# An encoder layer on one core: the later half of the in-projection in another order, the attention output loaded into its pages, and rows loaded after gates

## The chip, the cores and the metric

The kernel runs on one core of one Trainium2 chip. The metric is the device time of one execution in microseconds, as the median of several runs. Durations of single instructions come from one profiled execution.

## The reference, cut to what matters

One layer of a hybrid encoder over 2048 rows of 1024 features, in float32:

```
h  = rms_norm(x) * norm_mix
z  = h @ w_in          # q_a | k_a | v_a | q_b | k_b | v_b | gate_a | gate_b
y_a = windowed grouped-query attention of q_a, k_a, v_a
y_b = neighbourhood attention of q_b, k_b, v_b on a 32 x 64 grid
x  = x + (sigmoid(gate_a) * (y_a @ w_proj_a) + sigmoid(gate_b) * (y_b @ w_proj_b)) @ w_out
x  = x + relu(rms_norm(x) * norm_mlp @ w_up)^2 @ w_down
out = rms_norm(x) * norm_final
```

## The kernel before, in words

Every float32 operand is split into a high part, cast by ScalarE (L282 for most, L178 for a weight slice), and a low part, the rest, which VectorE subtracts (L283, L179). A product is then three matmuls of 128x512 (L286 to L288, or L202 to L204). The big products are done as seven block products (numbered 1 to 7, as in Strassen's scheme), whose operands are sums of blocks.

**In-projection.** h is kept transposed in "pages" of SBUF. QUADS lists groups of columns of w_in; each group (a "quad") does its seven products against the rows of one half of the sequence: quads 0 to 8 for the first half, quads 9 to 13 for the second. A quad of 256 columns has two groups of 12 matmuls per product, the one of 128 columns (O_KA) has one. After product 1 the bank is copied by ScalarE (L532), and product 6 goes on in the copy. Results leave through the three `ze` tiles to DRAM (`qs_a`, `qs_b`, `ks_a` and so on; L427 to L432 fill them, L452 stores). Beside quads 5 to 7 a generator `h1_sums` reads four slices of the second half's h back from DRAM (`h1d`), scales them on ScalarE (L552), sums on VectorE and stores through GpSimd. Beside quads 9 to 12, `wo_parts` prepares the blocks of w_out (`wo_d`).

**Attention.** Then come attention A and B. TensorE alternates between attention work (scores L1049, transposes L1077, products L1089) and "filler": gate tiles for the second half, then `proj_tiles`, which multiply y_a by w_proj_a. The transposed probabilities `pt` of attention B are cast by ScalarE (`phb`, L1083) and their rest taken by VectorE (`plb`, L1084). `paced` decides when the next piece of filler is issued. y_a is taken from DRAM by `y_page`: a 0.5 MB load into a `raw` tile (L940), then the cast L282 and the subtraction L283 into two pages.

**Gates and out-projection.** For each half m, `gated(f)`, f from 0 to 7, loads a row of gates and of A's product (`z`, L1544 and L1546), does 8 groups of 12 matmuls over two calls, combines on VectorE (L1553), and adds into m0 to m3 (L279). `out_products` then multiplies by w_out, with `pgl` tiles loaded from `wo_d` (L1451), copies four banks after product 1 (L1491) and adds the rest to rows of x (`xr`, loaded by `x_row`, 0.5 MB each, added by L279). At m = 1 the rows of m = 0 are normalised and turned beside the gates (`ht`, L249 and L254), and the first operands of the up-projection are prepared (`uraw`, `ubh`).

What sets the order: the program is built with a scheduler that takes each engine's instructions into one fixed order; an engine then works strictly in that order. `tc.issue_after(i)` tells it to place the enclosed instructions behind instruction i, without a wait of its own. DMAs are issued by the engine in whose order they stand, mostly SyncE (SP), some by ScalarE and GpSimd.

## Time and profile before

| what | us |
|---|---|
| median of 3 runs (2633.69 to 2640.96) | 2635.83 |
| the profiled execution, whole | 2633.67 |
| its span, first to last instruction | 2631.9 |
| TensorE busy (97%) | 2556.9 |
| VectorE busy (65%) | 1708.3 |
| ScalarE busy (50%) | 1308.2 |
| mean granted TensorE clock | 0.993 |

TensorE is busy for nearly the whole span, so what can be read from the profile are the places where it stands still, what it waits for there, and the granted clock around them. The views used are the waits by stage, tables of busy time by stretch, the chain of work in time order, and single rows of the timeline.

### The profile page before, as it was taken

The page shows a single profiled execution, that of the slowest core. Times are in us where ns is not written, and L with a number is a line of the kernel's source. Part 1 is how long each engine was busy: PE and PEld are TensorE (multiplying, and loading weights), DVE is VectorE, ACT ScalarE, POOL GpSimd, SP SyncE. Part 2 cuts the span into 40 slices and gives each one's busy share as a digit, 9 for nine tenths or more (in the row PEclk, how much of TensorE's full clock was granted, in tenths as well). Part 3 has the DMA queues.
Part 4 walks back from the last instruction along what each step waited for, and adds up shares of the span by engine and source line. Part 5 has one row for each costly group of instructions (what it writes and reads, how often), then busy time and mean ns, then how long its engine had stood idle before and what let it go on. Part 6 is the DMA issues. An engine that isn't in the chain of part 4 may idle for free.

```text
span 2631.9 us, 34511 instructions
## 1 busy us (share of the span) xinstructions
PE 2556.9 (97%) x11936; PEld 2123.0 (81%) x11936; DVE 1708.3 (65%) x2696; ACT 1308.2 (50%) x2345; POOL 335.1 (13%) x460
## 2 busy tenths in 40 slices
PE   8999999999998989989999999999999999999998
PEld 6877888878887878878777888888887888888887
DVE  7857476656664666656787677776656634554766
ACT  7365464567775666514246555644444322323444
POOL 1001001143445645200000000000000000000011
PEclk9999999999999989999999999999999999999999
DMA  5768578783358888797897655854427825444554
GB/s 184 224 181 296 163 246 269 256 246 113 96 150 207 228 250 233 232 330 245 266 331 248 232 209 199 284 199 145 155 97 291 313 102 183 147 145 168 184 195 165
DMA packets 348160, 553.22 MB, mean 210 GB/s; under 512 B 30904, under 2 KB 152888, under 8 KB 345808
## 3 DMA queue, kind: packets, MB, share of 16 engines
q1 hardware_dynamic: 333520, 515.35, 60.4%
q10 hardware_dynamic: 10944, 24.12, 2.5%
q0 software_dynamic: 3520, 11.54, 1.2%
q8 instruction: 94, 1.54, 0.2%
q14 instruction: 82, 0.67, 0.1%
HBM read 364.19 MB, written 186.71 MB: 209 GB/s over the span
## 4 chain that ended last, share of the span: by engine, by line
PE 78%; DMA 10%; DVE 6%; ACT 3%; issue 2%; SPq 2%; POOL 0%; DVEq 0%; ACTq 0%; POOLq 0%
PE b L287 16%; PE b L288 16%; PE b L286 16%; PE zb L286 5%; PE zb L288 5%; PE zb L287 5%; PE mm L202 2%; PE mm L204 2%; PE mm L203 2%; PE av L1089 1%; DMA h2d<-ht 1%; PE pt L863 1%; DMA y_b<-yb 1%; PE pt L1077 1%; PE s L1049 1%
## 5 line engine op out<-in xcount | busy, mean ns | idle before, releaser
L287 PE MATMUL b<-dwh,dah 128*128 128x512 f32 x896 | 348.7, 389 | 0.4 <-DVE dwh L283 0.4
L288 PE MATMUL b<-dwh,dah 128*128 128x512 f32 x896 | 347.8, 389 | 0.0
L286 PE MATMUL b<-dwh,dah 128*128 128x512 f32 x896 | 338.5, 389 | 1.7 <-ACT dwh L282 1.7
L282 ACT CAST dah<-da 128x1024 fp32r<-128x1024 f32 (+1 forms) x128 | 120.9, 945 | 367.4 <-PE b L288 246.7
L286 PE MATMUL zb<-zh,zwhl 128*128 128x512 f32 x728 | 286.2, 393 | 7.1 <-ACT zb L532 3.7
L287 PE MATMUL zb<-zh,zwhl 128*128 128x512 f32 x728 | 285.9, 393 | 0.0
L288 PE MATMUL zb<-zh,zwhl 128*128 128x512 f32 x728 | 284.0, 391 | 0.8 <-DVE zwhl L283 0.8
L283 DVE TENSOR_TENSOR dah<-da,dah 128x1024 fp32r<-128x1024 f32 (+1 forms) x128 | 139.2, 1089 | 217.5 <-ACT dah L282 215.8
L286 PE MATMUL b<-ubh,uwhlb 128*128 128x512 f32 x592 | 231.4, 391 | 5.1 <-ACT uwhlb L282 3.5
L287 PE MATMUL b<-ubh,uwhlb 128*128 128x512 f32 x592 | 231.0, 390 | 0.0
L288 PE MATMUL b<-ubh,uwhlb 128*128 128x512 f32 x592 | 229.1, 389 | 0.0
L286 PEld LDWEIGHTS b<-dwh,dah 128*128 128x128 f32 x896 | 168.1, 188 | 36.9 <-ACT dwh L282 2.1
L287 PEld LDWEIGHTS b<-dwh,dah 128*128 128x128 f32 x896 | 168.2, 188 | 35.8 <-DVE dwh L283 0.8
L288 PEld LDWEIGHTS b<-dwh,dah 128*128 128x128 f32 x896 | 168.2, 188 | 34.9
L279 DVE TENSOR_TENSOR uc<-b,uc 128x512 f32<-128x512 f32 x160 | 109.3, 689 | 119.4 <-PE b L288 112.8
L286 PEld LDWEIGHTS zb<-zh,zwhl 128*128 128x128 f32 x728 | 137.2, 188 | 39.6 <-ACT zb L532 4.9
L202 PE MATMUL mm<-zh,whl 128*128 128x512 f32 x368 | 158.5, 431 | 3.3 <-ACT z L470 2.2
L288 PEld LDWEIGHTS zb<-zh,zwhl 128*128 128x128 f32 x728 | 137.4, 189 | 29.7 <-DVE zwhl L283 1.6
L287 PEld LDWEIGHTS zb<-zh,zwhl 128*128 128x128 f32 x728 | 137.4, 189 | 27.6
L204 PE MATMUL mm<-zh,whl 128*128 128x512 f32 x368 | 146.1, 397 | 0.0
L203 PE MATMUL mm<-zh,whl 128*128 128x512 f32 x368 | 146.0, 397 | 0.0
L286 PEld LDWEIGHTS b<-ubh,uwhlb 128*128 128x128 f32 x592 | 111.5, 188 | 29.7 <-ACT uwhlb L282 3.9
(254 smaller groups left out, 5678.7 us busy)
## 6 DMA issues: line engine op xcount, KB each, us to landing
at<-uc SPq DMA_DIRECT2D x224, 256.0 KB
da<-at SPq DMA_DIRECT2D x96, 512.0 KB
dw<-in_w_down_dram SPq DMA_DIRECT2D x160, 256.0 KB
uraw<-in_w_up_dram SPq DMA_DIRECT2D x32, 1024.0 KB
pgl<-wo_d SPq DMA_DIRECT2D x28, 1024.0 KB
zraw<-in_w_in_dram SPq DMA_DIRECT2D x24, 1024.0 KB
z<-zg SPq DMA_DIRECT2D x64, 256.0 KB
qs_a<-ze SPq DMA_DIRECT2D x32, 256.0 KB
```

What stands on the lines that cost most here:

```text
L202: PE.matmul(ps, lh, rh, start=first, stop=False)
L203: PE.matmul(ps, lh, rl, start=False, stop=False)
L204: PE.matmul(ps, ll, rh, start=False, stop=last)
L279: return eng.tensor_tensor(out=out, in0=a, in1=b, op=op).ins
L282: A.copy(hi, src)
L283: return eng.tensor_tensor(out=lo, in0=src, in1=hi.bitcast(F32), op=ALU.subtract).ins
L286: PE.matmul(ps, lh, rh, start=first, stop=False, skip_group_check=True)
L287: PE.matmul(ps, lh, rl, start=False, stop=False, skip_group_check=True)
L288: PE.matmul(ps, ll, rh, start=False, stop=last, skip_group_check=True)
L863: last = PE.transpose(pt[:, h * P : (h + 1) * P], s[:, h, c * P : (c + 1) * P], ident).ins
L1049: PE.matmul(ps[:, :n], q[:, i, :], kv[:, z, B_R0[i] // 4 : (B_R0[i] + B_NR[i]) // 4, 4 * B_C0[j] : 4 * (B_C0[j] + w)], start=z == 0, stop= ...
L1077: last = PE.transpose(pt[:kp, at + (i - i0) * P : at + (i - i0 + 1) * P], s[i][:, rr : rr + kp], ident)
```

## The change

Five edits:

1. `h1_sums` runs beside quads 6 and 7 (two slices each, two steps per product) and no longer beside 5; `wo_parts(0)` runs beside quad 5, and the others, 1 to 3, beside the quads of 256 columns of the second half.
2. The second half's quads are QA, KA, KB, VB, QB in place of QA, QB, KB, VB, KA.
3. `y_page` becomes `y_pages`, called for two pages at once when the last gate tile of a page is done. It loads y_a straight into the low page, casts to the high page (L948) and subtracts in place (L949). Casts and subtractions stand behind the attention-B cast that is four ahead of the one due then (`casts`, `now`).
4. `casts` and `now` are kept in `attn_b` and `paced`.
5. In `gated`, the last load of A's product is kept, and the first two operands of the out-projection (`pgl`) at f = 3 and each row of x from f = 4 on stand behind it.

```
-    QUADS += [(O_QA, 256), (O_QB, 256), (O_KB, 256), (O_VB, 256), (O_KA, P)]
+    QUADS += [(O_QA, 256), (O_KA, P), (O_KB, 256), (O_VB, 256), (O_QB, 256)]
...
         if q == 5:
-            prep = h1_sums(0)
-        elif q == 6:
-            prep = h1_sums(1)
-        elif q == 7:
-            prep, steps = in_turn((h1_sums(2), h1_sums(3))), 2
+            prep = wo_parts(0, own)
+        elif q in (6, 7):
+            k = 2 * (q - 6)
+            prep, steps = in_turn((h1_sums(k), h1_sums(k + 1))), 2
...
-        elif q >= SECOND:
-            prep = wo_parts(q - SECOND, own)
+        elif q >= SECOND and QUADS[q][1] == 256:
+            n_wo[0] += 1
+            prep = wo_parts(n_wo[0], own)
...
+                if f == 15:
+                    y_pages(0 if b == 3 else 2)
...
-    def y_page(b):
-
-        hi, lo = (in_page[(6, 3, 1, 2)[b]]() for _ in range(2))
-        for g in range(2):
-            raw = T(wp, [P, KC, P], F32, "raw", 3).rearrange("p (c a) t -> p c (a t)", c=2)
-            SY.dma_start(raw, y_a[g][:, b * BT : (b + 1) * BT].rearrange("(c p) t -> p c t", p=P))
-            split(raw, halves(hi)[g], halves(lo)[g], V)
-        ypages[b] = hi, lo
+    def y_pages(b0):
+
+        for b in (b0, b0 + 1):
+            ypages[b] = [in_page[(6, 3, 1, 2)[b]]() for _ in range(2)]
+            for g in range(2):
+                SY.dma_start(halves(ypages[b][1])[g].bitcast(F32),
+                             y_a[g][:, b * BT : (b + 1) * BT].rearrange("(c p) t -> p c t", p=P))
+        with tc.issue_after(casts[min(now[0] + 4, len(casts) - 1)]):
+            for b in (b0, b0 + 1):
+                for h, l in zip(*map(halves, ypages[b])):
+                    A.copy(h, l.bitcast(F32))
+                    V.tensor_tensor(out=l, in0=l.bitcast(F32), in1=h.bitcast(F32), op=ALU.subtract)
...
-                SY.dma_start(ga[:, j], zp[2 * m + j][f])
+                last_dma[0] = SY.dma_start(ga[:, j], zp[2 * m + j][f]).ins
...
             if f == 3:
-                ready = [next(operands), next(operands)]
+                with tc.issue_after(last_dma[0]):
+                    ready = [next(operands), next(operands)]
             if f >= 4:
-                rows[0].append(x_row(m, 0, f % 4))
+                with tc.issue_after(last_dma[0]):
+                    rows[0].append(x_row(m, 0, f % 4))
```

The edits move instructions on every engine. Three places show how.

**SyncE at the start of the gates, m = 0.** Names: `z<-zg` are loads of gate rows, `z<-zp` loads of A's product, `zp<-z` stores of it, `xr` rows of x, `pgl` blocks of w_out, `yraw` y_b, `raw` a slice of w_proj_b. Before, from the third row load on, up to the gate row of f = 1 (z_11721):

```order
L217 DMA xr_11963<-in_x_dram 128x1024
L217 DMA xr_12000<-in_x_dram 128x1024
L1451 DMA pgl_11832<-wo_d_964 128x2x1024
L217 DMA xr_12012<-in_x_dram 128x1024
L175 DMA zp_121<-z_11360 128x512
L217 DMA xr_12014<-in_x_dram 128x1024
L217 DMA xr_12088<-in_x_dram 128x1024
L217 DMA xr_12090<-in_x_dram 128x1024
L1142 DMA yraw_12234<-y_b_146 128x512
L1142 DMA yraw_12238<-y_b_147 128x512
L189 DMA raw_12568<-in_w_proj_b_dram 128x4x128 x2
L1544 DMA z_11721<-zg_99 128x512
```

With the change, from the weight slice on (z_11713 is the gate row of f = 1, the four loads after it are those of f = 2):

```order
L189 DMA raw_12560<-in_w_proj_b_dram 128x4x128 x2
L1551 DMA z_11713<-zg_99 128x512
L1551 DMA z_11713<-zg_101 128x512
L1551 DMA z_11754<-zg_99 128x512
L1551 DMA z_11754<-zg_101 128x512
L1553 DMA z_11755<-zp_108 128x512
L1553 DMA z_11755<-zp_116 128x512
L1551 DMA z_11789<-zg_99 128x512
L1551 DMA z_11789<-zg_101 128x512
L1553 DMA z_11790<-zp_109 128x512
L1553 DMA z_11790<-zp_117 128x512
L1458 DMA pgl_11824<-wo_d_964 128x2x1024
```

The eight loads of rows of x and a block of w_out that stood ahead of the gate row of f = 1 stand behind those of f = 1 to 3.

**ScalarE in attention B, where the pages of y_a are cast.** `phb<-pt` is the attention's cast, `zh<-raw` a page's cast from a loaded tile. Before, a stretch with two of the eight page casts:

```order
L1083 CAST phb_9166<-pt_9161 128x512
L282 CAST zh_1400_10932<-raw_10938 128x1024
L1083 CAST phb_9179<-pt_9174 128x512
L282 CAST zh_1406_10990<-raw_10992 128x1024
L1083 CAST phb_9191<-pt_9187 128x384
L1057 ACTIVATE stb_9211<-stb_9211 128x4
L1083 CAST phb_9248<-pt_9244 128x384
```

With the change, the first four page casts (`zh<-zh`, from the low page itself):

```order
L1090 CAST phb_8755<-pt_8751 96x384
L1103 COPY yb_7484<-av_8655 64x512
L1090 CAST phb_8768<-pt_8763 96x512
L948 CAST zh_1083_9066<-zh_1084_9067 128x1024 x2
L948 CAST zh_1085_9070<-zh_1086_9071 128x1024 x2
L1090 CAST phb_8781<-pt_8776 96x512
L178 CAST whl_9009<-raw_9006 128x1024
L470 ACTIVATE z_9037<-mm_9082,bg 128x512
L1090 CAST phb_8793<-pt_8789 96x384
```

The eight page casts, once spread singly between attention casts, stand in two runs of four, the second of them behind the cast of a later unit (phb_9353).

**ScalarE at the start of the quad after QA, in the second half.** `ze` are tiles of QA on their way to DRAM, `zwhl` weight casts, and the copy L532 is the one after product 1 of the new quad. Before, with QB next:

```order
L282 CAST zwhl_3312<-zS_3310 128x1024
L431 ACTIVATE ze_3231<-zc_3115 128x512
L282 CAST zwhl_3318<-zS_3316 128x1024
L431 ACTIVATE ze_3249<-zc_3129 128x512
L431 ACTIVATE ze_3271<-zb_3048 128x512
L431 ACTIVATE ze_3288<-zb_3063 128x512
L532 COPY zb_3351<-zb_3338 128x512
L282 CAST zwhl_3321<-zraw_3033 128x1024
L532 COPY zb_3366<-zb_3353 128x512
```

With the change, with KA next, whose weight casts are half as wide:

```order
L431 ACTIVATE ze_3252<-zc_3139 128x512
L282 CAST zwhl_3352<-zS_3350 128x4x128
L431 ACTIVATE ze_3275<-zc_3159 128x512
L282 CAST zwhl_3358<-zS_3356 128x4x128
L431 ACTIVATE ze_3293<-zc_3173 128x512
L282 CAST zwhl_3361<-zraw_3077 128x4x128
L431 ACTIVATE ze_3315<-zb_3092 128x512
L431 ACTIVATE ze_3332<-zb_3107 128x512
L532 COPY zb_3391<-zb_3378 128x512
L282 CAST zwhl_3364<-zraw_3075 128x4x128
L535 COPY zc_3406<-zb_3393 128x512
```

The copy still stands behind all of QA's `ze` rows; what has changed is the quad whose product 6 uses it.

More of the change, by code (lines that the diff above doesn't have):

```diff
@@ L754, in in_turn @@
             yield from g
-    right2 = {}
+    right2, n_wo = {}, [0]
     for q in range(2, len(QUADS)):
@@ L904, in paced @@
                 at = len(marks) - 1
+            now[0] = max(at, 0)
             with tc.issue_after(marks[at]) if at >= 0 else nullcontext():
@@ L930, in gate_tiles @@
                 put(zg[b][f // 8][(f % 8) * P : (f % 8 + 1) * P, :], zs[f][:, b - 2])
+                if f == 15:
+                    y_pages(0 if b == 3 else 2)
                 yield
     ypages = [None] * NB
[L935 to L942 removed]
+    def y_pages(b0):
[9 more added lines that the diff above has]
+                    V.tensor_tensor(out=l, in0=l.bitcast(F32), in1=h.bitcast(F32), op=ALU.subtract)
+    casts, now = [], [0]
     def proj_tiles(f):
@@ L1082, in attn_b @@
             pl = T(bp, [P, 512], F32R, "plb", 3)
-            A.copy(ph[:kp, :at], pt[:kp, :at])
+            casts.append(A.copy(ph[:kp, :at], pt[:kp, :at]).ins)
             V.tensor_tensor(out=pl[:kp, :at], in0=pt[:kp, :at], in1=ph[:kp, :at].bitcast(F32), op=ALU.subtract)
```

2 lines of the change are left out of this document (removed).

## The prediction

> **What bounds the kernel now.** I first read the page's busy times:
>
> ```profile
> span 2631.9 us, 34511 instructions
> ...
> PE 2556.9 (97%) x11936; PEld 2123.0 (81%) x11936; DVE 1708.3 (65%) x2696; ACT 1308.2 (50%) x2345; POOL 335.1 (13%) x460
> ```
>
> TensorE stands still for 2631.9 - 2556.9 = 75 us in all. The change removes no matmul, so it can win only from these 75 us and from time in which TensorE ran at a lower clock. Next, therefore, a table by stretch (start and end, length, then busy time and number of instructions of PE, its weight loads, DVE, ACT and POOL; granted TensorE clock; busy share of the DMA engines; GB/s):
>
> ```profile
> 217.00:222.00 5.00, 4.83 (x14) 3.74 (x15) 4.73 (x5) 5.00 (x7) 0.49 (x1) 0.66 0.25 91
> 540.00:906.00 366.00, 350.56 (x1911) 296.11 (x1911) 230.00 (x642) 244.39 (x647) 175.85 (x235) 1.00 0.60 166
> 880.00:906.00 26.00, 26.00 (x165) 23.50 (x164) 15.78 (x45) 18.25 (x47) 16.65 (x20) 1.00 0.70 194
> 906.00:980.00 74.00, 65.07 (x357) 55.44 (x356) 46.22 (x102) 47.51 (x109) 34.27 (x41) 0.91 0.88 250
> 1130.00:1190.00 60.00, 52.56 (x222) 42.66 (x221) 35.45 (x43) 11.96 (x14) 0.00 (x0) 0.94 1.01 354
> 1135.50:1151.90 16.40, 16.40 (x73) 13.33 (x71) 5.73 (x6) 2.11 (x2) 0.00 (x0) 1.00 1.01 379
> 1158.30:1163.20 4.90, 4.82 (x12) 3.83 (x13) 4.78 (x7) 1.05 (x1) 0.00 (x0) 0.55 1.10 349
> 1260.00:1345.00 85.00, 78.20 (x333) 62.99 (x333) 68.22 (x94) 27.76 (x41) 2.19 (x4) 0.98 0.88 303
> 1322.80:1328.70 5.90, 5.78 (x18) 4.63 (x19) 4.63 (x5) 4.60 (x7) 0.00 (x0) 0.71 1.05 374
> ```
>
> Three stretches that the change touches idle most: 906 to 980 (8.9 us, where y_a is cast), 1130 to 1190 (7.4 us, gates of m = 0), 1260 to 1345 (6.8 us, gates of m = 1). The idle time of 540 to 906 is large too, but in the changed program every engine's order there is that of before, so I leave it. The table also shows a second cost. From 1135.5 to 1151.9, 73 matmuls take 16.40 us, 0.225 us each, at clock 1.00. Right behind the wait, 12 take 4.82 us at 0.55, where 12 x 0.225 = 2.7 would do: **a wait here costs its own length and some 2.1 us of slow matmuls**. The same after 217 (14 matmuls, 4.83 against 3.15: 1.7 us) and after 1322.8 (18, 5.78 against 4.05: 1.7 us).
>
> [...]
>
> **Sums a quad later.** The chain and the timeline around 215:
>
> ```profile
> 198.59 15.30 DMA xin<-h1d
> ```
> ```profile
> 213.97 1.15 ACT L552 ACTIVATE xin<-xin,g_mix 128x1024 f32<-128x1024 f32 x1 [6.57 <-DMA xin<-h1d]
> ...
> 216.53 0.58 ACT L532 COPY zb<-zb 128x512 f32<-128x512 f32 x1
> ```
>
> ScalarE stood 6.57 us at the scaling of a slice whose load took 15.30 us; the copy that TensorE needed was behind it, and TensorE went on at 217.17, after 2.1 us of waiting. The sums' scaling now comes a quad later, and the copy no longer has it ahead. **-2.1 - 1.7 = -3.8.** What moves with it: per slice four loads on SP, two scalings on ScalarE, four sums on VectorE and four stores on GpSimd, now twice as densely beside quads 6 and 7; w_out's loads take their place beside 5. At the next quad change the copy is close to its use:
>
> ```profile
> 258.49 0.57 ACT L532 COPY zb<-zb 128x512 f32<-128x512 f32 x1 [0.31 <-DVE ze L428]
> ```
> ```profile
> 259.68 0.39 PE L286 MATMUL zb<-zh,zwhl 128*128 128x512 f32 x1
> ```
>
> TensorE's first matmul in that copy starts 0.6 us after it ends. Denser sums could use this up, by nothing or by as much as the wait removed (2.1 us); I give it 0.3, since the scalings stand some copies away. Term: **-3.5** (-3.8 to -1.5).
>
> **Order of columns.** Attention A begins with q_A of the second half:
>
> ```profile
> PE s L844 <- DMA qa<-qs_a: 3.3, 1, 3.3
> ```
> ```profile
> 543.46 6.24 DMA qa<-qs_a
> ```
>  The waits view (total, times, longest) gives 3.3 us for it. In the new order the qa loads are still behind the last stores of the last quad on SP, but some 72 matmuls (16 us at 0.225) separate those stores from their use, against 6.24 us of loading: the 3.3 go, and the rows show no slow clock behind them. The price is at the other end:
>
> ```profile
> 402.22 0.39 PE L286 MATMUL zb<-zh,zwhl 128*128 128x512 f32 x1
> ```
> ```profile
> 409.54 0.60 ACT L431 ACTIVATE ze<-zb 128x512 fp32r<-128x512 f32 x1 [0.67 <-DMA qs_a<-ze]
> 410.04 0.59 ACT L532 COPY zb<-zb 128x512 f32<-128x512 f32 x1
> ```
>
> The next quad's product 1 starts at 402.22. The copy after it stands on ScalarE behind QA's `ze` rows, the last of which waits for a store to leave one of the three tiles, and ends at 410.63, 8.4 us after that start. Before, products 1 and 5 of QB (two groups of 12 each, 4 x 12 x 0.225 = 10.8 us) came ahead of its use. KA has one group in each, 5.4 us, and the `ze` rows are as many. So TensorE waits 8.4 - 5.4 = 3.0 us, and with a slow clock of 1.6 behind it 4.6. Bounds: 0, if the stores land sooner beside KA's smaller weight loads, and 4.6. I take 4.3. Term: -3.3 + 4.3 = **+1** (-3.3 to +1.3).
>
> **Pages of y.** ScalarE's groups and the chain in 906 to 980:
>
> ```profile
> L1083 ACT CAST phb<-pt 96x384 fp32r<-96x384 f32 (+3 forms) x26 | 13.4, 527 | 7.5 <-PE pt L1077 7.4
> L282 ACT CAST zh<-raw 128x1024 fp32r<-128x1024 f32 x8 | 8.4, 1050 | 14.7 <-DMA raw<-y_a 14.1 <-PE mm L203 0.6
> ```
> ```profile
> 916.39 5.47 DMA raw<-y_a
> ...
> 936.23 10.33 DMA raw<-y_a
> ...
> 959.28 6.69 DMA raw<-y_a
> ```
>
> Eight casts wait 14.1 us for loads of y_a; the `phb` casts and TensorE wait behind them. The stretch loses 8.9 us idle and 65.07 x (1 - 0.91) = 5.9 us of clock: 14.8. With the change the loads are issued when a page is free and the casts stand four `phb` casts later. Those come 26 in 71 us, 2.7 us apart, so the casts come some 11 us after the load's issue; the slowest load above took 10.33. I take the loads as just landed. Then a run of four casts costs 4 x 1.05 = 4.2 us of ScalarE between two `phb` casts of 0.53. Between the two `pt` groups' uses TensorE has about 34 matmuls, by the stretch 880 to 906 (165 in 26.00 us) 5.4 us, against 0.53 + 4.2 + 0.53 and some 0.5 us for the signal: about 0.4 us short. VectorE's subtractions of the same four, in one queue with `plb`, add about as much as one of them, 1.1 us. So 1.5 us a run, with the slow clock 3.1; two runs, 6.3. Term: 6.3 - 14.8 = **-8.5** (0, if loads stay late, to -14.8).
>
> What stands behind the page loads on SP, which wait for TensorE to be done with a page, are loads of q, v and bias for the coming units of attention B; see the rivals.
>
> **Rows behind gates, m = 0.** The wait, and the chain before it:
>
> ```profile
> PE b L202 <- DVE z L1553: 6.4, 1, 6.4
> ```
> ```profile
> 1139.60 9.99 DMA zp<-z
> ```
> ```profile
> 1149.60 7.95 DMA z<-zg
> ```
>
> TensorE waited 6.4 us for L1553, which waited for the gate row of f = 1. That load was issued at 1149.60 because SP stood behind eight `xr` of 0.5 MB and a `pgl` of 1 MB, at 379 GB/s some 13 us of transfer. They now stand behind it. It still needs the store of a `z` tile to land (the store of the tile before it, issued about 1136.6, then about four transfers of 0.25 MB at 0.7 us), so I see it issued near 1141 and landed near 1144; the product that it meets is ready at 1143.5. The wait goes: -6.4 - 2.1 = -8.5. What is late next: the bytes are the same and the DMA share is 1.01, so rows of x and `pgl` end up to 6 us nearer to their uses; counted from 1141 at 379 GB/s, the 15.6 MB up to the last row land near 1182, about when the first out-product begins, and rows are used later still. I leave 0.5 for it. Term: **-8** (-8.5 to 0).
>
> **The same at m = 1.** The waits of 1260 to 1345, and single rows:
>
> ```profile
> PE b L286 <- DVE xr L279: 2.9, 2, 1.7
> PE b L202 <- DVE z L1553: 2.0, 2, 1.6
> PE b L286 <- ACT b L1491: 1.9, 1, 1.9
> ```
> ```profile
> 1320.39 1.99 ACT L282 CAST ubh<-uraw 128x1024 fp32r<-128x1024 f32 x2 [3.64 <-DMA uraw<-h2d]
> ```
> ```profile
> 1330.78 1.42 DVE L249 STREAM_TRANSPOSE ht<-xr 128x256 f32<-128x256 f32 x4
> 1332.12 1.18 DVE L283 TENSOR_TENSOR ubh<-uraw,ubh 128x1024 fp32r<-128x1024 f32 x1
> ```
>
> The four copies L1491 stood behind the `ubh` casts, which waited 3.64 us for a load, and TensorE waited 1.9. In the new order three copies stand ahead of the casts, the fourth behind, and it is used 4 us later than the first. The additions to `xr` stood behind these turns and two `ubh` subtractions on VectorE (1.42 + 1.18 + 1.22 = 3.8 us), and TensorE waited 2.9 for them; turns and subtractions now stand behind the additions. Sum 4.8, the shorter wait on L1553, 0.4, and the clock's 1.7: 6.9. The longer one, 1.6, stays, since VectorE's rows ahead are the same. As this stage's order is most shuffled, I keep 1.4 back. Term: **-5.5** (-8.5 to 0).
>
> **Sum.** -3.5 + 1 - 8.5 - 8 - 5.5 = -24.5, against the profiled execution's 2633.67: 2609.2. That execution lies 2.2 below the median shown and at the lower edge of its runs (2633.69 to 2640.96), so I add some 2: **2611 us**.
>
> **Rivals.**
> - **The casts cost as much in runs as spread** (2620): if loads in 906 to 980, DMA share 0.88, take longer than 11 us, ScalarE stands four casts deep. Then -8.5 becomes 0. For it: 10.33 us is close to 11. Against it: four loads no longer wait for `raw` tiles.
> - **The slow matmuls stay** (2616): those after 217 and 1322, and the 2.7 us counted in 906 to 980, do not come from the short waits ahead of them, and go on when these are gone. The terms lose 1.7 + 1.7 + 2.7, and KA's price its 1.3: net 4.8. Against it: 0.66 and 0.71 stand right behind waits of about 2 us. [...]
> - **The transfers are the limit** (2628, no change that can be told): with the DMA share at 1.01 around 1140, another load is late in place of the gate row, and with 0.88 at 906 to 980 the pages are too. Then both -8 and -8.5 go.
> - **Slower: SP stands at the page loads** (2648). The four page loads wait for TensorE to be done with the pages; SP works in order, and attention B's q, v and bias loads behind it are late. Each of four waits could cost up to a load's 10.33 us less the 2.7 of one cast's distance, 7.6: 30 in all, and the -8.5 is gone: 2611 + 8.5 + 30 = 2649.5, less what overlaps. It makes the kernel slower by over 0.3% once a wait costs (24.5 - 8.5 + 8)/4 = 6 us. Against it: those loads were issued some units ahead before.
> - **More than forecast** (2600): KA's wait doesn't come and the casts cost nothing.
>
> **How the numbers follow.** 0.3% of 2635.83 is 7.9 us, about what a measurement can tell from no change: 2627.9 and 2643.7. Chances: forecast 0.42, casts 0.18, slow matmuls 0.14, transfers 0.14, SP 0.08, more 0.04. Faster: 0.42 + 0.18 + 0.14 + 0.04 = 0.78; same 0.14; slower 0.08. The range runs from 2600 to 2632: it leaves out the slower case and a part of the outer ones.
>
> **What would show it.** Right: no wait of L202 on L1553 above 1 us and clock 1.00 over the gates of m = 0; no wait on `qa`; a wait of some 3 us at a copy L532 near 407; in 906 to 980 fewer than 5 us idle, on `phb` and `plb` behind L948, none of them ended by a page load. Wrong: L948 waiting on y_a, waits on `qb`, `vb` or `kb` after 906, or on `xr` or `pgl` after 1180.

## The result, and the profile after

| | before | changed |
|---|---|---|
| median, us (12 runs each) | 2638.82 | 2636.88 |
| range, us | 2633.69 to 2643.06 | 2629.99 to 2643.57 |
| ratio, 95% interval | | 0.9994, 0.998 to 1.0008 |
| span of the profiled execution, us | 2631.9 | 2635.7 |
| TensorE busy, us | 2556.9 | 2555.2 |
| mean granted clock | 0.993 | 0.992 |

The forecast was 2611 us, a gain of 1%; what came is no difference that the runs can tell. Yet most of the waits that the change aimed at are gone. The page of the changed kernel, and its table by stretch for the three stages that the prediction led with (busy time and number of instructions of PE, weight loads, DVE, ACT and POOL, then clock, DMA share, GB/s):

```profile
span 2635.7 us, 34520 instructions
...
PE 2555.2 (97%) x11936; PEld 2123.7 (81%) x11936; DVE 1712.1 (65%) x2696; ACT 1307.6 (50%) x2345; POOL 342.0 (13%) x460
```
```profile
906.00:980.00 74.00, 65.13 (x379) 57.39 (x378) 49.27 (x108) 47.15 (x107) 39.76 (x42) 0.93 0.99 271
1130.00:1190.00 60.00, 58.45 (x259) 48.10 (x258) 40.07 (x48) 14.81 (x18) 0.00 (x0) 1.00 0.96 338
1260.00:1345.00 85.00, 79.21 (x336) 63.48 (x335) 62.72 (x89) 26.63 (x40) 2.19 (x4) 0.98 0.85 284
```

From 1130 to 1190 TensorE now stands still for 1.5 us where it was 7.4, and its clock is 1.00. From 906 to 980 it still stands for 8.9 us, exactly as before, though it gets through 379 matmuls in place of 357. From 1260 to 1345 it is 5.8 us, after 6.8. So one of the three stages was cured, and its gain must have gone somewhere. The waits right behind it and in the pages' stage (total, times, longest):

```profile
PE b L286 <- DMA pgl<-wo_d: 4.9, 1, 4.9
PE mm L202 <- DVE z L970: 1.5, 1, 1.5
```
```profile
PE av L1096 <- DVE plb L1091: 6.1, 3, 3.4
PE s L1056 <- DVE stb L1061: 1.6, 3, 0.8
PE av L1096 <- ACT phb L1090: 1.2, 1, 1.2
```

The first pair is from 1125 to 1215: the wait of 6.4 us on L1553 is gone, and a wait of 4.9 us for a block of w_out stands at 1200 in its place. The second group is from 906 to 985: ScalarE's page casts (L948) have no idle time ahead of them any more, as forecast, but 6.1 us of TensorE's waiting are ended by VectorE's `plb`. The waits between 400 and 560:

```profile
PE s L844 <- DVE ze L428: 3.0, 1, 3.0
PE zb L286 <- ACT zb L532: 2.5, 1, 2.5
```

The wait of 2.5 us at KA's copy was forecast. The one of 3.0 us in front of attention A was not: in the place of `qa` (3.3) attention A now waits for VectorE to empty the last quad's banks, and that last quad is QB, with twice KA's columns.

**How far one trace can be trusted.** Kernels differ in their profiles by some microseconds even in stages that no edit touches. So all stage lengths below are taken between the same two matmuls of TensorE (found by their number), as differences to the profile of before. For instance, from the matmul at 402 to the one at 605, thirteen kernels with the same order there (those without edits 1 and 2, before among them) are 0.0 to 6.7 us longer than the profile of before, 3.4 on average; from 985 to 1061, ten kernels without the pages' edit are 0.0 to 4.3 longer, 2.7 on average. Before's own profile is the shortest in both. The 2633.67 us on which the prediction made its sum was an execution in which these two stages went well by chance, some 6 us together; the median of 2638.8 lies 5 us above it.

### The profile page after: what moved, and what is told of

Read it like the earlier page. It is cut to its first block, busy times and chain, and to the rows that moved or that the text cites. A ratio compares the mean times of both kernels' runs of the same rounds, so it can differ in the third digit from the quotient of the medians.

```text
span 2635.7 us, 34520 instructions
## 1 busy us (share of the span) xinstructions
PE 2555.2 (97%) x11936; PEld 2123.7 (81%) x11936; DVE 1712.1 (65%) x2696; ACT 1307.6 (50%) x2345; POOL 342.0 (13%) x460
## 4 chain that ended last, share of the span: by engine, by line
PE 43%; DVE 3%; DMA 2%; SPq 1%; ACT 1%; issue 0%; POOL 0%; POOLq 0%; DVEq 0%; ACTq 0%
PE b L287 14%; PE b L288 14%; PE b L286 14%; SPq L257 1%; DMA dw<-in_w_down_dram 0%; DMA uraw<-h2d 0%; DVE xr L279 0%; DVE uraw L279 0%; DMA at<-uc 0%; DMA x2d<-xr 0%; DVE ubh L283 0%; DVE pgl L283 0%; DMA uraw<-in_w_up_dram 0%; DMA x<-x2d 0%; DVE uc L279 0%
```

## Experiments

All ratios are to the kernel before, from runs on the same chip, with 95% intervals. "Stage" is the difference as just defined.

**One edit at a time.** Each kernel is the one before with one part of the change.

```
e1_sums:   edit 1 (sums beside quads 6 and 7, wo_parts(0) beside 5, the others behind SECOND)
e2_order:  edit 2 (QA, KA, KB, VB, QB)
e3_pages:  edits 3 and 4 (y_pages, casts, now)
e4_gates:  edit 5 (pgl and rows of x behind the loads of A's product)
```

> Before with edit 1 alone (sums a quad later, w_out's parts beside quads 5, 9, 10, 11). Theory 'given back at once': quad 5 is about 4 us shorter than before (the wait of ScalarE on the slice is gone), and quads 6 and 7 are together about 3 us longer, because the denser sums delay the copies and transposes there; the start of quad 8 stands within 1 us of before, and the time is that of before within noise. Rival 'the edits collide': alone, edit 1 wins its 3.5 us and quads 6 and 7 are as before.

> Before with edit 2 alone (QA, KA, KB, VB, QB). Theory 'given back at once': a wait of 2.5 us at the copy L532 beside KA with some 1.5 us of slow matmuls behind it, and attention A begins as late as before or later, now behind VectorE's last ze of QB (about 3 us) in place of the load of qa; attention A starts 3 to 5 us later than before. Rival 'the edits collide': the wait on VectorE's ze comes from another edit, alone the time to attention's start is that of before within 1 us.

> Before with edits 3 and 4 alone (y loads into the pages, casts in two runs of four). Theory 'the runs block VectorE': two waits on plb L1091 behind the subtractions L949, 2 to 3.5 us each, none on a load of y_a; from 906 to 1060 the program gains about 4 us on before. Rival 'late loads': L948 waits for y_a and the gain is under 1 us. My forecast had 8.5 us.

> Before with edit 5 alone (first w_out blocks and rows behind the gates). Theory 'the queue is paid later': the wait of 6.4 us at the gate of f = 1 is gone (about 8.5 us with the clock), and a wait of some 5 us for a pgl load (w_out, product 2) comes at the start of the out-projection, 7 us with the clock; at m = 1 within 2 us of before. Rival 'late because of the other edits': without them the gates start at another phase of the queue, the pgl wait does not come, and 8 us stay won.

| kernel | median, us | ratio | interval | stages that the edit touches |
|---|---|---|---|---|
| e1_sums | 2639.92 | 1.0 | 0.9986 to 1.0015 | 204 to 246: -4.0; 246 to 326: +3.6 |
| e2_order | 2639.0 | 0.9993 | 0.9983 to 1.0002 | 402 to 605: +4.0 (without the edit 0.0 to 6.7) |
| e3_pages | 2637.79 | 0.9986 | 0.997 to 1.0003 | 920 to 985: -2.3 (without -6.1 to +3.3) |
| e4_gates | 2638.49 | 0.9996 | 0.9985 to 1.0008 | 1135 to 1163: -8.6; 1163 to 1209: +8.6 |

No part gives more than 0.15%, and none is measurably slower: the expected gains fail one by one. For the sums the waits view from 195 to 340 shows it, first before, then e1_sums:

```profile
PE zb L286 <- ACT zb L532: 2.1, 1, 2.1
PE zb L286 <- DVE zc L279: 0.6, 1, 0.6
```
```profile
PE zb L286 <- DVE zc L279: 1.2, 1, 1.2
PE zb L397 <- DVE ze L411: 1.2, 1, 1.2
PE zb L397 <- ACT zc L457: 0.8, 1, 0.8
```

The copy's wait is gone; the transposes of V (L397) now wait for ScalarE and VectorE, which do two slices' sums in the time of one. These two waits make 2.0 of the 3.6 us that 246 to 326 is longer; the rest stands in no single wait of the view. Over all four kernels with this edit the stretch from 204 to 326 is -0.5 us on average, over fourteen without it -0.5 as well.

e3_pages did not come out as expected. The first run of casts made the expected wait on `plb`, 2.2 us. But the casts of the second run stood 3.7 us for two loads of y_a (one landed 12.2 us after its issue), and TensorE waited 5.1 us for the `phb` behind them:

```profile
PE av L1096 <- ACT phb L1090: 5.1, 1, 5.1
```
```profile
L948 ACT CAST zh<-zh 128x1024 fp32r<-128x1024 f32 x8 | 8.0, 1049 | 3.7 <-DMA zh<-y_a 3.7
```

So the rival "late loads" is half true here, while in the changed kernel the same loads landed in time. e2_order has both waits of its theory without any other edit (2.4 us at the copy, 3.0 us on `ze`), but its +4.0 lies within what kernels without the edit show.

e4_gates is the clearest. The same stage, no other edit, and the 8.6 us that it wins up to 1163 are paid by 1209:

```profile
PE b L286 <- DMA pgl<-wo_d: 5.5, 1, 5.5
```

**Which of the two gates, and why is the operand late?** The late transfer is the fourth `pgl`, the second block of `wo_d` for product 2. SyncE's rows ahead of it in the changed kernel:

```profile
1183.03 0.33 SPq L217 DMA_DIRECT2D xr<-in_x_dram  x1
1183.69 1.01 SPq L1551 DMA_DIRECT2D z<-zg  x2
1185.10 1.63 SPq L189 DMA_DIRECT2D raw<-in_w_proj_b_dram  x2
1187.67 2.03 SPq L1149 DMA_DIRECT2D yraw<-y_b  x2
1190.22 1.56 SPq L1553 DMA_DIRECT2D z<-zp  x2
1192.17 1.04 SPq L1149 DMA_DIRECT2D yraw<-y_b  x2
1193.76 1.18 SPq L1551 DMA_DIRECT2D z<-zg  x2
1195.34 1.30 SPq L1553 DMA_DIRECT2D z<-zp  x2
1196.68 0.43 SPq L1551 DMA_DIRECT2D z<-zg  x1
1197.46 0.37 SPq L1458 DMA_DIRECT2D pgl<-wo_d  x1
```

The last row of x is issued at 1183.03, then fifteen transfers of 0.25 MB, all for m = 1 and used after 1260, then at 1197.46 the operand, which lands at 1204.72. I first took this for SyncE's own waiting: it stood 3.2 and 1.9 us for a tile of the two-deep ring of A's product, with nothing else to issue. Of the next four runs two try the ring, one takes the gates apart, one moves them.

```
e5_xr      before, only x_row under tc.issue_after(last_dma[0])
e8_early   before, m = 0 only:  pgl behind loads[1], x_row behind loads[f - 2]
e9_ring    changed kernel:  T(p4, [P, 2, BT], F32, "z", 3)  in place of 2
e16_ring   before, with that ring alone
```

> The kernel before with only the rows of x placed behind the gates' loads; the first two pgl stand where they stood. Theory (the late second operand, waited for 4.9 us near 1200, is the price of the pgl and rows that were moved, since SyncE has nothing to issue while it stands before the two-deep ring of z): the gate row of f = 1 has 1 MB of pgl, 2.8 us at 379 GB/s, ahead of it and is met by a wait of 0 to 3 us at 1145 to 1155 (6.4 before), and a wait on pgl near 1200 stays but is shorter, 1 to 4 us, since one block of w_out is already through. Rival (only the pgl gate makes operands late): no wait on pgl above 1 us near 1200. Second rival (the place of the rows doesn't matter to the wait at 1152): 6 us there again. Time: within 0.3% of the kernel before in any case; what tells is the row at 1152 and that at 1200.

> The kernel before with pgl and rows of x at m = 0 behind the loads of two steps earlier than in the change (pgl behind those of f = 1, the row of f behind those of f - 2); m = 1 is as before. Theory (time lost near 1200 was SyncE standing idle with transfers held back behind loads that wait for the two-deep ring): SyncE has rows to issue between those loads, the wait on pgl near 1200 falls from 4.9 us to below 1 us, and the wait at 1152 stays below 3 us (one pgl of 1 MB is ahead of the gate row of f = 1: 2.8 us at 379 GB/s); 1135 to 1209 then takes 5 to 9 us less than in the kernel before. Rival (the bytes are the limit: what must land before 1200 is the same, so any order pays the same): whatever is gained at 1152 is paid again by 1209, and the stretch is within 1.5 us of the kernel before. Time: 2632 to 2636 by the theory, 2637 to 2641 by the rival.

> The changed kernel with a third tile in the ring that takes A's product in the gates (2 before). Theory (SyncE stood 3.2 and 1.9 us for a tile of that ring, and the operand of w_out behind it landed some 5 us late): SyncE's waits on the additions into m0 to m3 between 1130 and 1200 go to under 1 us, the transfers don't pause, and the wait on pgl near 1200 falls from 4.9 us to below 2 us; 1135 to 1209 takes 4 to 6 us less than in the changed kernel. Rival (the operand is late because 13 MB of other transfers are ahead of it): SyncE waits less, but the wait on pgl near 1200 stays within 1.5 us of 4.9. Time: 2632 by the theory, 2636.9 by the rival.

> The kernel before with the third tile in the ring for A's product and nothing else. In the run with this ring and the rows two steps early the time was 0.9962 of before; the changed kernel with this ring was at 0.9964, the rows two steps early alone at 0.9963. Theory (the gain near 1150 to 1209 comes from where pgl and rows of x stand among the gates' loads): the ring alone leaves the wait at 1152 (5 us or more) in place and gains nothing, ratio 0.9985 to 1.0015. Rival (the ring itself gives the gain, by letting loads of A's product go ahead in all sixteen steps): ratio 0.995 to 0.9975, and less waiting on L1553 or L1554 between 1260 and 1300.

| kernel | median, us | ratio | interval | 1135 to 1163 | 1163 to 1209 | sum | fourth operand lands after the stage's first matmul |
|---|---|---|---|---|---|---|---|
| before | | | | 0 | 0 | 0 | 64.9 |
| changed | 2636.88 | 0.9994 | 0.998 to 1.0008 | -8.7 | +7.3 | -1.4 | 64.9 |
| e5_xr | 2640.03 | 0.9989 | 0.9969 to 1.0008 | -8.7 | +8.0 | -0.7 | 65.4 |
| e8_early | 2632.5 | 0.9963 | 0.9945 to 0.9982 | -8.7 | +3.8 | -4.9 | 61.9 |
| e9_ring (5 runs) | 2632.74 | 0.9964 | 0.9944 to 0.9983 | -8.7 | +9.6 | +0.9 | 67.0 |
| e16_ring | 2637.15 | 0.9994 | 0.9981 to 1.0006 | +2.1 | 0.0 | +2.1 | 68.3 |

In e9_ring TensorE's wait is the longest of all, and my theory of the ring is dead:

```profile
PE b L286 <- DMA pgl<-wo_d: 7.0, 1, 7.0
```

e16_ring agrees: the ring alone leaves the wait on L1553 (8.6 us there) and gains nothing. (That e9_ring's ratio is below that of the changed kernel isn't explained by this stage, nor by any that I found; with five runs it stays open.) e8_early gains 4.9 us in the stage, close to the 5 to 9 of its theory, though a wait of 1.9 us for the operand stays.

The last column shows what holds instead: **in all six kernels the fourth operand lands 62 to 68 us after the stage begins.** TensorE, if it never waits, needs it after 1199.86 - 1139.86 = 60.0 us, the start of its wait in the changed kernel less the stage's first matmul. e5_xr says the same of the two gates: with the rows of x alone moved the wait at 1152 is gone, a `pgl` of 1 MB ahead of the gate row costs nothing, and the operand is still waited for, 5.4 us.

The six don't land there for one and the same reason, though. The ring of `pgl` holds three operands, so the fourth can't be loaded before TensorE is done with the first. That is 49.1 us after the stage's first matmul where TensorE hasn't waited, but 57.8 in before and 60.0 in e16_ring, where it has; and there SyncE issued the load right then, at 57.9 and 60.0. In these two TensorE's own lateness explains the landing. In the four kernels with a gate the place was free at 49.1, and SyncE issued at 57.6 (changed), 58.0, 53.8 and 59.1: there the transfers ahead on the queue made it late. That before and the changed kernel both have 64.9 is thus chance, and whether a second lateness already stood behind before's wait of 6.4 us no run shows. The table by stretch shows what the transfers did: the first 20 us of the stage, then the next 40, of before, the changed kernel and e4_gates.

```profile
1135.50:1155.50 20.00, 16.51 (x73) 13.33 (x71) 5.73 (x6) 2.11 (x2) 0.00 (x0) 1.00 1.03 373
1155.50:1195.50 40.00, 37.12 (x155) 30.54 (x156) 30.96 (x37) 11.50 (x15) 0.00 (x0) 0.91 1.01 350
```
```profile
1139.90:1159.90 20.00, 20.00 (x90) 16.58 (x89) 12.88 (x15) 3.17 (x3) 0.00 (x0) 1.00 0.89 292
1159.90:1199.90 40.00, 39.96 (x177) 32.78 (x175) 27.29 (x31) 12.89 (x17) 0.00 (x0) 1.00 1.06 380
```
```profile
1148.40:1168.40 20.00, 20.00 (x90) 16.56 (x88) 12.48 (x14) 3.16 (x3) 0.00 (x0) 1.00 0.81 258
1168.40:1208.40 40.00, 40.00 (x177) 32.84 (x175) 27.37 (x31) 13.10 (x17) 0.00 (x0) 1.00 1.05 375
```

TensorE is perfect in these 60 us of the changed kernel (20.00 of 20.00, 39.96 of 40.00), and the transfers are what falls back: 292 GB/s in the first 20 us, since rows and operands are held behind loads that wait for VectorE, where before had 373. Then they are full, 380. 20 us at 292 GB/s are 5.8 MB, 40 us at 380 are 15.2: 21.0 of the 23.0 MB that the trace has from the stage's first matmul to the operand's landing. At 380 throughout, 23.0 MB take 60.5 us, by which estimate, with the same loads ahead of it, the operand would land when it is needed and no earlier, even without a pause. e8_early and e15_early_ring (below) let rows go two steps sooner, and the first 20 us of the latter read:

```profile
1140.40:1160.40 20.00, 20.00 (x90) 16.57 (x89) 10.04 (x13) 3.16 (x3) 0.00 (x0) 1.00 0.98 339
1160.40:1200.40 40.00, 39.99 (x177) 32.79 (x175) 30.65 (x35) 14.03 (x19) 0.00 (x0) 1.00 1.03 375
```

339 for 292, and the operand lands 3 us sooner.

**Moving m = 1 out of the way.** If transfers for m = 1 stand ahead of the operand, hold them back.

```
+    wo_loads = []
+    def later(m):
+        return tc.issue_after(wo_loads[3]) if m else nullcontext()     # e13: wo_loads[7]
...
+                with later(m):   around the loads of y_b, slices of w_proj_b, gate rows, A's product
```

e10_fourth and e13_eighth are the kernel before with edit 5 and this; e11_mend and e14_spread8 add the pages with spread casts (next part), and e12_all adds edit 1 to e11_mend.

> The kernel before with rows behind gates as in the change, and the loads that m = 1 issues ahead of time (gate rows, A's product, weight slices, y_b) placed behind the fourth operand of the out-projection of m = 0. Theory (with the transfers full from 1155 on, the fourth operand of w_out lands late because ten loads of 0.25 MB of rows and four of y_b for m = 1, used after 1260, stand ahead of it on SyncE; the two-deep ring is not the cause, since a third tile left the wait at 7.0 us): the fourth operand is issued 8 to 10 us earlier, the wait on pgl near 1200 falls below 1 us, none above 1 us takes its place by 1260, and 1135 to 1209 keeps the 8.7 us that the removed wait at 1152 gives. Rival (all transfers are the limit, whatever their order: another operand, a row of x, y_b or a row of m = 1 is late in its place): 5 us or more of waits on pgl, xr, y_b or gate rows between 1187 and 1345. Time by the theory 8 us below the kernel before (ratio 0.997), by the rival as the kernel before.

> The kernel before with rows behind gates, and the loads that m = 1 issues ahead of time placed behind the eighth operand of the out-projection of m = 0 in place of the fourth. Theory (from 1155 on the transfers are full, so an operand's wait goes only if what is moved behind it is not itself ahead of another operand; behind the fourth, the sixth became late by 5.6 us because some twenty loads of m = 1 stood ahead of it): all operands land before their use, no wait on pgl above 1 us between 1187 and 1260, and the 8.7 us that the removed wait at 1152 gives are kept up to 1264. The rows and y_b of m = 1 then land near 1240, ahead of their use at 1262. Rival (the transfers owe the time somewhere: what is held back longest is late in turn): 5 us or more of waits on gate rows, y_b or weight slices of m = 1 between 1255 and 1300. Time by the theory 6 to 9 us below the kernel before, ratio near 0.997; by the rival ratio 0.999 to 1.001.

| kernel | median, us | ratio | interval | 1135 to 1209 | 1209 to 1264 |
|---|---|---|---|---|---|
| e10_fourth | 2641.03 | 1.0003 | 0.9989 to 1.0017 | -8.7 | +10.3 |
| e13_eighth | 2637.95 | 0.999 | 0.9978 to 1.0002 | -8.7 | +13.5 |

The fourth operand now lands 54 us after the stage's begin and is never waited for, but the time is lost one step further on. Waits of TensorE from 1187 to 1260 in e10_fourth, and of SyncE from 1175 to 1215; then TensorE's from 1187 to 1264 in e13_eighth:

```profile
PE b L286 <- DMA pgl<-wo_d: 5.6, 1, 5.6
PE b L286 <- DVE xr L279: 1.6, 1, 1.6
```
```profile
SPq L1457 <- PE b L288: 8.2, 1, 8.2
```
```profile
PE b L286 <- DMA pgl<-wo_d: 6.4, 2, 3.4
PE b L286 <- ACT xr L237: 2.0, 1, 2.0
```

In e10_fourth SyncE stood 8.2 us, from 1181.9 to 1190.1, for the fourth's place in the ring, with everything for m = 1 behind it; the transfers were busy for 0.66 of that time, and the moved loads then stood ahead of the sixth operand. Its rival holds: what is held back is late in turn. In e13_eighth neither expectation holds as it stands: between 1255 and 1345 no load for m = 1 is waited for, but from 1234 on later blocks of w_out (6.4 us) and a row of x behind ScalarE (2.0 us) are.

**The pages in spread form.** In the changed kernel the eight casts of the pages come as two runs of four. VectorE around the first run:

```profile
938.07 2.35 DVE L949 TENSOR_TENSOR zh<-zh,zh 128x1024 fp32r<-128x1024 f32 x2
940.35 0.55 DVE L1061 CUSTOM_DVE_ANT_0 sb<-s,biass 128x384 f32<-128x384 f32 x1
940.82 0.08 DVE L1061 DVE_READ_ACCUMULATOR2_ANT stb<- 128x1 f32 x1
940.82 0.45 DVE L1061 CUSTOM_DVE_ANT_0 sb<-s,biass 128x288 f32<-128x288 f32 x1
941.20 0.08 DVE L1061 DVE_READ_ACCUMULATOR2_ANT stb<- 128x1 f32 x1
941.20 2.35 DVE L949 TENSOR_TENSOR zh<-zh,zh 128x1024 fp32r<-128x1024 f32 x2
943.47 0.68 DVE L1091 TENSOR_TENSOR plb<-pt,phb 96x512 fp32r<-96x512 f32 x1
```

From 938.07 to 943.47 VectorE does four subtractions of 1.2 us and two score rows, and the next `plb` comes behind them all; TensorE stood 2.15 us for it and went on at 944.21, 0.06 us after its end. e7_spread is e3_pages with each cast, and its subtraction, behind an attention cast of its own:

```
+        n = now[0] + 4
         for b in (b0, b0 + 1):
             for h, l in zip(*map(halves, ypages[b])):
+                with tc.issue_after(casts[min(n, len(casts) - 1)]):
                     A.copy(h, l.bitcast(F32))
                     V.tensor_tensor(out=l, in0=l.bitcast(F32), in1=h.bitcast(F32), op=ALU.subtract)
+                n += 1
```

> The kernel before with the pages edit, but each of the eight casts of a page (and its subtraction) behind an attention cast of its own in place of two runs of four. Theory (what eats the gain between 906 and 980 is that four subtractions of 1.2 to 1.6 us stand in one queue on VectorE ahead of plb): the waits of L1089 on plb, 2 to 3 us each behind the runs, fall below 1 us each, and from 906 to 980 TensorE stands idle for under 5 us, where the runs cost 8 or 9; the stage gets 3 to 6 us shorter than in the profile with the runs, and casts do not wait for y_a. Rival (the subtractions and casts themselves are too many for the stage, wherever they stand): idle time stays at 8 us, spread over more waits of 1 us. Second rival (spread casts come too early for the loads): waits of L948 on y_a of over 2 us come back. Time 2630 to 2637 by the theory, 2635 to 2642 by the rivals, which the spread of runs hardly tells apart; the stage does.

> The same, with the pages edit in its spread form (each cast of a page behind an attention cast of its own). Theory (the two gains are in different stages and add): 906 to 985 takes some 9 us less than in the kernel before, 1135 to 1209 some 8.7 less; of the first, 0 to 8 us come back in waits for vb between 985 and 1061, as they did in the run with spread casts alone (7.7 us). Time 8 to 17 us below the kernel before, ratio 0.9935 to 0.997. Rival (a faster stage only brings the next load's wait forward, since transfers are nearly full from 985 on): ratio 0.997 to 1.0, with waits on vb, kb or the gates' rows that add up to what was gained.

> The same, with the sums a quad later as well; of the five edits only the order of columns is left out. Theory (the sums give back beside quads 6 and 7 what they win beside quad 5, +3.6 against -4.0 in the run with that edit alone): no difference to the kernel without the edit that a measurement shows, under 2 us; between 204 and 326 under 1 us of difference to the kernel before. Rival (what is given back depends on chance, and the 4 us stay): 4 us less, 0.15%.

> The same, with the pages edit with each cast behind an attention cast of its own. Theory: 906 to 985 is 8 to 11 us shorter than in the profile of before, 2 to 8 of them come back as waits for vb between 985 and 1061, and 1135 to 1264 is 8 us shorter: 8 to 15 us below the kernel before, ratio 0.994 to 0.997. Rival (vb's loads take back all of the stage's gain, as they did with the spread casts alone): ratio 0.997, as without the pages.

| kernels | 920 to 985 | 985 to 1061 | sum |
|---|---|---|---|
| ten without the edit, mean | -1.5 | +2.7 | +1.1 |
| in runs: changed, e3_pages, e9_ring | -3.1, -2.3, -3.0 | -0.8, +6.4, -1.1 | -4.0, +4.1, -4.1 |
| spread: e7_spread, e11_mend, e12_all, e14_spread8, e17_both | -11.2, -8.7, -12.2, -10.6, -11.2 | +11.4, +9.7, +10.3, +10.8, +9.0 | +0.3, +1.0, -1.9, +0.2, -2.2 |

Times: e7_spread 2639.88 us, ratio 0.9993 (0.9979 to 1.0007); e11_mend 2637.94, 0.9997 (0.9983 to 1.001); e12_all 2637.07, 0.9992 (0.9981 to 1.0002); e14_spread8 2635.23, 0.9983 (0.997 to 0.9995). e12_all differs from e11_mend by edit 1 alone, and by less than 1 us. e11_mend's rival holds: with waits on `vb` (6.2 us) and on `pgl` behind it, the two gains don't show. e14_spread8's 0.17% is less than its theory asked for. The stage itself becomes what the prediction hoped for; from 920 to 985, the kernel before, then e7_spread:

```profile
920.00:985.00 65.00, 56.52 (x306) 47.82 (x305) 41.80 (x92) 38.38 (x86) 30.44 (x36) 0.89 0.85 251
```
```profile
920.00:985.00 65.00, 61.01 (x378) 53.62 (x377) 49.32 (x109) 47.24 (x109) 41.13 (x43) 1.00 0.97 268
985.00:1061.00 76.00, 67.66 (x398) 60.21 (x397) 44.92 (x114) 39.26 (x102) 34.55 (x44) 0.93 0.84 225
```

378 matmuls for 306, clock 1.00 for 0.89. And the next 76 us give it back, since the loads of `vb` for attention B don't come sooner (e7_spread, 985 to 1065):

```profile
PE av L1098 <- DMA vb<-vs_b: 7.7, 2, 5.5
```

All five kernels show it. SyncE stands for stores of `z` to land between 960 and 1050 (33 us in e7_spread, 30 before), with `vb` behind; that this is what fixes the pace is argued from the rows, no run took it away.

**What beats both.** e15_early_ring is the kernel before with the rows two steps early (m = 0) and the third ring tile; e17_both adds the pages with spread casts.

> The kernel before with pgl and rows of x at m = 0 behind the loads of two steps earlier, and a third tile in the ring for A's product. Each of the two was measured alone at 0.996 of the kernel before, though the traces show only 1 to 5 us of difference within the edited stages, and in both the fourth operand of w_out still lands 62 to 67 us after the stage begins, as in every kernel so far but the one that moved it. Theory (those two ratios were mostly the spread between runs): ratio 0.998 to 1.0, fourth operand 61 to 67 us after the first matmul of the stage, wait on pgl near 1200 of 2 to 6 us. Rival (the gains are real and independent): ratio 0.992 to 0.995.

> The third tile, the rows two steps early and the pages edit with each cast behind an attention cast of its own. Theory (the pages' stage gains 8 to 10 us between 906 and 985, of which waits on vb take back 7 to 11 between 985 and 1061, as in each of the runs with spread casts): within 2 us of the run without the pages, ratio 0.995 to 0.997. Rival (the loads of vb are late by chance, and part of the gain stays): ratio 0.992 to 0.9945.

| kernel | median, us | ratio | interval | 1135 to 1209 |
|---|---|---|---|---|
| e15_early_ring (9 runs) | 2629.86 | 0.9962 | 0.9947 to 0.9976 | -6.7 |
| e17_both (5 runs) | 2627.37 | 0.9955 | 0.9943 to 0.9968 | -6.8 |

The three kernels with early rows are 4.9 to 6.8 us shorter in the stage than before's profile, where six kernels without edit 5 are 0 to 2.1 us longer (0.9 on average). That is some 7 us of gain, and the lower ends of the ratios' gains, 0.24% and 0.32% or 6.3 and 8.4 us, agree, with 1 to 3 us from the pages in e17. My theory for e15, that the ratios of 0.996 were chance, was wrong: for e8 and e15 they are real. The rival, that ring and early rows add, asked for 0.992 to 0.995 and isn't borne out either, though e15's stage is 1.8 us shorter than e8's. e17's theory holds: 0.9955, 0.07% below e15. The wait for the fourth operand is still there, and short, in e15:

```profile
PE b L286 <- DMA pgl<-wo_d: 1.7, 1, 1.7
```

## Why the prediction was wrong, step by step

| term | forecast, us | measured |
|---|---|---|
| sums a quad later | -3.5 | 0.0 (-0.5 with, -0.5 without, 204 to 326) |
| order of columns | +1 | +0.2 (3.7 with, 3.4 without, 402 to 605) |
| pages of y | -8.5 | -1.3 (-2.8 with, -1.5 without, 920 to 985) |
| rows behind gates, m = 0 | -8 | -1.2 (-0.3 with, 0.9 without, 1135 to 1209) |
| the same, m = 1 | -5.5 | +0.9 (0.0 with, -0.9 without, 1264 to 1432) |
| sum | -24.5 | -1.4 |

Means over kernels with and without each edit (e5_xr counts as one with edit 5); the sum of -1.4 us is a ratio of 0.9995, and 0.9994 was measured. Each mean rests on 3 to 14 profiles that differ by up to 7 us, so a single term below some 2 us can't be told from nothing; what is told is that none of the large gains is there.

- **Rows behind gates, m = 0.** The first step was right: the wait went, and its slow matmuls too, -8.7 us in every kernel with the gate. The step that failed is "What is late next ... I leave 0.5 for it". I counted 15.6 MB up to the last row of x, and saw it landed near 1182; it landed at 1191.44, since 17.7 MB came from 1141 to then and the transfers paused early (292 GB/s). And I stopped counting at that row: fifteen transfers for m = 1 and the fourth operand stood behind it. TensorE waited 4.9 us for that operand, and 1163 to 1209 became 7.3 us longer where 0.5 had been left. With the fifteen held back (e10_fourth, e13_eighth) the operand landed in time. The rival "transfers are the limit" described this half, "another load is late in place of the gate row", and I gave it 0.14.
- **Pages of y.** The loads no longer hold the casts up in the changed kernel, as forecast (the groups view has no idle time ahead of L948); in e3_pages two were late by 3.7 us in all, so "I take the loads as just landed" held by a narrow margin. The failed step is the price of a run of four, "So 1.5 us a run, with the slow clock 3.1". I let ScalarE's four casts and one of VectorE's subtractions count; in truth all four subtractions, 1.2 to 1.6 us each, stand ahead of `plb` in VectorE's queue. The first run cost a wait of 2.15 us, the second 1.20 (for ScalarE's `phb`) + 3.36, some 3.4 a run on average, and the clock went to 0.57 from 942 to 950. The 0.5 us "for the signal" in the sum is shown by no row; behind the `plb` above it was 0.06. e7_spread confirms that the runs are the cause: with them taken apart the stage is 8 us shorter than in the changed kernel. As it spreads the casts too, it doesn't part VectorE's share from ScalarE's; that VectorE's is the larger is read from the changed kernel's waits, 5.5 us on `plb` against 1.2 on `phb`. It also shows a second error, which no run of the change reached: attention B's next loads keep their own pace, and take it back.
- **Sums.** The wait of 2.1 us and its slow matmuls went, -4.0 where -3.8 was computed. "I give it 0.3" for two slices beside one quad was wrong: 3.6. I looked for the next copy at the next quad change; what became late were V's transposes inside the quads.
- **Order of columns.** The term came out near its value by luck: two errors cancel. KA's wait was as computed, 2.5 us for 3.0, and the 1.6 of slow clock came behind it: half of the 3.11 us of work from 410.46 to 413.87, where the clock was 0.50. The wait on `qa` did go, but one of 3.0 us on VectorE took its place, with slow matmuls behind it (clock 0.50 from 554.6 to 559.6): I had put 72 matmuls between QB's stores and attention A, and forgot that the scores need QB's PSUM banks emptied first. The other error is in "the rows show no slow clock behind them" for `qa`. That was so in the one profile at hand; thirteen kernels with the same order there have a wait of 2.1 to 4.3 us on `qa`, and in all but before's a clock of 0.50 to 0.70 follows it over 5 us. So the wait that went was worth more than 3.3.
- **m = 1.** "three copies stand ahead of the casts, the fourth behind, and it is used 4 us later than the first": the fourth was waited for, 2.1 us where all four had cost 1.9, so this gain did not come. The additions to `xr` ceased to be late, and the waits on the gates' combination came to 2.4 us where they had been 2.0.
- **The base.** The sum was made against 2633.67 and 2 us were added for the median. That execution was quick by some 5 us against the median of 2638.82, so even a perfect sum would have come out some 3 us low.

What was right: the waits at the copy near 215, on `qa`, on L1553 at m = 0 and on `xr` at m = 1 went, and two prices that a stage shows by itself (-3.8 near 215, -8.5 at 1152) came out within 0.3 us. What failed in the sums, the order and the gates of m = 0 is the same step, the wait that was second in line; in the pages it is the price of a run of casts, at m = 1 the place of one copy. The rival that came nearest is "transfers are the limit": its half on the gates happened, its half on the pages not in the changed kernel, and its 2628 lies 9 us below the median measured.

## What to carry to other kernels

A wait that ends last can hide the ones behind it: before counting it as a gain, take the next transfer or engine on the same path, and work out when it would be ready if TensorE came earlier by the whole wait; if the transfers are full, count every byte ahead of it on its queue, those for later stages too, and look when its place in the ring comes free. When a helper moves work to ease one engine, list what it now stands ahead of in the other engine's queue: a run of four casts is also a run of four subtractions. And where the gain sought is 0.3% or less, judge a stage by the time between the same two instructions in several kernels, not by two profiles.

## What the runs showed of the hardware

**Run to run.** One program on one chip takes 2633 to 2649 us (26 runs of before beside e5 to e9), 0.6% between the ends, and on another 2627 to 2650 (31 runs beside e1 to e4). The stages without an edit that differ most between the traces hold waits for transfers (402 to 605, 906 to 1061); that these make the spread of the runs is not shown, since each kernel has one trace.

**Slow matmuls after waits.** In the 18 profiles, from 66 us on, TensorE waited longer than 1.1 us 332 times. Of waits of 1.1 to 1.7 us, 12 of 172 were followed by a granted clock below 0.9 over the next 5 us; of 1.7 to 2.3 us, 28 of 41; of 2.3 to 3.3, 31 of 42; of 3.3 to 4, 41 of 45; above 4, all 32. So in these profiles a wait's second price was seldom paid below 1.7 us, by 100 of the 128 waits from 1.7 to 4, and by every wait above 4. Its size is told by the traces' records of the clock: in before and the changed kernel, between 66 and 2600 us, the granted clock is 1.0 or 0.5, and of the 16 stretches at 0.5 ten last 3.41 us and six 6.83. The price is half of what TensorE works in them: in before 1.7 us from 217.26 to 220.67, and 2.2 for the 4.38 us of work in 1155.93 to 1162.76, where the prediction had counted 1.7 and 2.1 from matmuls. Of two waits for the same operand, of nearly the same length, the first was not followed by slow matmuls and the second was: e15_early_ring behind 1.69 us, then e8_early behind 1.89.

```profile
1202.00:1207.00 5.00, 4.92 (x22) 4.07 (x23) 5.00 (x6) 0.73 (x2) 0.00 (x0) 1.00 1.03 411
```
```profile
1205.02:1210.02 5.00, 5.00 (x15) 3.98 (x16) 3.94 (x5) 0.72 (x2) 0.00 (x0) 0.66 1.01 400
```

22 matmuls against 15 in the same 5 us. The prediction's rival that the slow matmuls don't come from the waits is refuted: in each of the kernels where the wait at 1152 went, the clock from 1135 to 1163 was 1.00, and 0.83 to 0.88 in each where it stayed.
